# Hybrid decoder trunk: a silu behind a cast, an adaLN load behind a group's loads, two columns beside one output tile

## The chip, the cores and the metric

The kernel runs as one program on one core of a Trainium2 chip. The metric is the device time of one execution in microseconds (us). Before the change the median of three runs is 1824.08 us, from 1823.46 to 1824.4.

The core has five engines that take instructions from queues of their own, each in its program's order: TensorE (PE, matrix products; PEld are its weight loads), VectorE (DVE), ScalarE (ACT), GpSimd (POOL) and SyncE (SP). They wait for each other by semaphores. In this kernel SP and POOL mainly issue DMAs, whose packets share 16 DMA engines.

## The reference, cut to what matters

Two layers, each a SwiGLU feed-forward (FFN), a token mixing, and a second FFN; D = 1024, 512 tokens, all in float32. Only the FFNs (w_in 1024 x 5632, w_out 2816 x 1024) and the adaLN modulation are touched; the mixing is left out here:

```python
c_act = jax.nn.silu(c)
for l in range(DEPTH):
    mod = (c_act @ w_ada[l] + b_ada[l]).reshape(B, N_MOD, D_MODEL)
    sh1, sc1, gt1, sh2, sc2, gt2, sh3, sc3, gt3 = [mod[:, i, None, :] for i in range(N_MOD)]
    hn = rms_norm(h, g_ffn1[l]) * (1.0 + sc1) + sh1
    h = h + 0.5 * (1.0 + gt1) * swiglu(hn, w_ffn1_in[l], w_ffn1_out[l])
    ...
    hn = rms_norm(h, g_ffn2[l]) * (1.0 + sc3) + sh3
    h = h + 0.5 * (1.0 + gt3) * swiglu(hn, w_ffn2_in[l], w_ffn2_out[l])

def swiglu(x, w_in, w_out):
    gate, up = jnp.split(x @ w_in, 2, axis=-1)
    return (jax.nn.silu(gate) * up) @ w_out
```

## The kernel before

**Products.** A float32 weight `w` is split into two parts that PE takes at its fast rate: `wH`, a rounded copy that ACT makes (L130), and `wL = w - wH`, a subtraction on DVE (L132). Activations are split in the same way (hnH and hnL, actH and actL, comH and comL). Each product is three matmuls: H by H, L by H, H by L (L118 to L120, or L414 to L416).

**An FFN** (`ffn`, L333) has 22 hidden tiles of 128, in pairs 0 to 10. They are worked in two groups, pairs 0 to 5 and pairs 6 to 10; after each group the output projection adds that group's share to the residual h.

- The first pairs are *classical*: for each of their tiles PE makes the gate (`pg`) and the up product (`pu`), ACT applies silu to the gate (L495), DVE multiplies (L497), and the result is split. There are two such pairs, four in the first FFN of layer 0.
- Beside these tiles DVE forms sums and differences of the rows and column halves of hn, called P1, P2, T3 and T4 (`combine`). Each is a tile `q` that is split at once: cast to comH on ACT, subtraction to comL on DVE. `when` says beside which tile each is made.
- The other pairs (`pair_in`) save multiplications in the manner of Strassen: each makes products of sums of weight blocks with those sums of rows, 24 matmuls of 256 columns each. A pair loads the blocks A(1,0), as `sum0` or `sum1` by turns, with A(1,1) added to it by an accumulating DMA on POOL (L366); A(0,0) as `first`; A(0,1) as `wraw`, also called a12; A(0,0) again as `third`, with A(1,0) added by POOL; and A(1,1) as `wraw`. DVE adds `first` and later `wraw` into the sum (L356). The product with P2 goes into the accumulator `ps_d` only when ACT has copied it out (`s`, L440). In ACT's queue the cast of `third` and the copy `up` (L436) stand ahead of that copy. The product T4 of each pair is put off into the next pair.
- An output tile i (eight in group 0; six and the last two in group 1) multiplies the group's hidden tiles by two loaded pieces of w_out (w1o or w2o, 384 KB in group 0 and 320 KB in group 1). In group 0 the pieces go into `wraw` buffers or into `sum0`.

**adaLN beside it.** The matrix w_ada is too large to go through PE: a column block of 128 x 1024 is loaded by POOL (L202, `wada`, 512 KB) and DVE multiplies it by `crep`, silu(c) repeated over the partitions, and sums along the row (L188). `ada_steps` does a few of them beside each output tile. The `wada` tiles share the buffers `first`, `third` and `sum1` with the pairs' weights: the first pair of group 1 can load its own blocks only when the dots that read these buffers are done. `crep` is loaded by SP (L192) and goes through silu on ACT (L193), once in each FFN.

**What sets the order.** A scheduler fixes each engine's order of instructions when the program is built, by priority in the order of the code and by its own estimate of times. `tc.issue_after(x)` makes what is issued inside it stand behind instruction x. SP and POOL issue DMAs in order: one that waits for its buffer holds up all behind it.

Of the kernel before, what the change touches and what calls it, by code (L numbers as in the profile page):

```python
# [8 lines left out]
F32 = mybir.dt.float32  # L9
F32R = mybir.dt.float32r  # L10
I32 = mybir.dt.int32
AF = mybir.ActivationFunctionType
# [5 lines left out]
P = 128  # L18
D = 1024
# [40 lines left out]
def trunk_kernel(ctx, tc, ins, out, layers=L, phases=("ffn1", "mix", "ffn2")):  # L60
    nc = tc.nc
# [11 lines left out]
    act, mm = nc.scalar.activation, nc.tensor.matmul  # L73

    def E(name="e", dt=F32):
        return sp.tile([P, T], dt, name=name, tag="e", bufs=4)
# [7 lines left out]
    def psmm(tags=("mm",)):  # L84
        turn[0] += 1
        return psum([P, T], "ps_mm", tags[turn[0] % len(tags)])
# [27 lines left out]
    def mm3(acc, w, k, x, sl, start, stop):  # L114

        wH, wL, xH, xL = w[0][:, k], w[1][:, k], weave(x[0][:, sl]), weave(x[1][:, sl])
        acc = paired(acc)
        mm(acc, wH, xH, start=start, stop=False)  # L118
        mm(acc, wH, xL, start=False, stop=False)  # L119
        latest["large"] = mm(acc, wL, xH, start=False, stop=stop)  # L120

    latest = {}

    def queue_behind(name):
        return tc.issue_after(latest[name].ins) if name in latest else nullcontext()

    def split(hi, lo, src, behind=None):
        a, d = behind or (None, None)
        with queue_behind(a):
            nc.scalar.copy(hi, src)  # L130
        with queue_behind(d):
            return nc.vector.tensor_sub(lo, src, hi.bitcast(F32))  # L132

# [31 lines left out]
    def prm(l, name):  # L165
        a, b = PAR[name]
        return par[:, l, a:b]
# [15 lines left out]
    ada_turn = [0]  # L183
    todo = [(l, i, k) for l in range(layers) for i in range(9) for k in range(KD)][2 * KD :]

    def ada_dot(out_, w, crep):

        stt(w, w, 1.0, crep, ALU.mult, ALU.mult, accum_out=out_)  # L188

    def ada_crep(pool):  # L190
        c = pool.tile([P, D], F32, name="crep", tag="crep", bufs=1)
        nc.sync.dma_start(c, ins["crep"])  # L192
        act(c, c, AF.Silu)  # L193
        return c

    def ada_steps(pool, crep, n, behind=None):

        cols = []
        for l, i, k in todo[:n]:
            ada_turn[0] += 1  # L200
            w = pool.tile([P, D], F32, name="wada", tag=("first", "third", "sum1")[ada_turn[0] % 3], bufs=1)
            nc.gpsimd.dma_start(w, ins["wadaT"][l, i, k])  # L202
            cols.append(w)
        with tc.issue_after(behind.ins) if behind else nullcontext():
            for m, (w, (l, i, k)) in enumerate(zip(cols, todo)):
                if (l, i) not in mod:
                    mod[l, i] = const.tile([P, KD], F32, name=f"mod{l}_{i}")
                ada_dot(mod[l, i][:, k : k + 1], w, crep)
                k0 = k if m == 0 or k == 0 else k0
                if k == KD - 1 or m == len(todo[:n]) - 1:  # L210
                    v = mod[l, i][:, k0 : k + 1]
                    tt(v, v, prm(l, "b_ada")[:, i * KD + k0 : i * KD + k + 1], ALU.add)
        del todo[:n]

    def ada_until(pool, crep, l, i):
        while todo and todo[0] <= (l, i, KD - 1):
            ada_steps(pool, crep, 1)
# [60 lines left out]
    loads = []  # L278
# [43 lines left out]
    def residual(pt, i, gate, ss, sl=ALL):  # L322
        hs = inorder(h[i][:, sl])
        done = stt(hs, Woven(pt).view, gate[:, i : i + 1], hs, ALU.mult, ALU.add)
        add_ss(ss, i, sl)
        return done
# [6 lines left out]
    def ffn(l, w_in, w_pair, w_out, hn, im, ss, need, then, first, ready, coming):  # L333
# [6 lines left out]
        with tc.tile_pool(name="act", bufs=1) as ap_:  # L340
            com = {n: tuple(ap_.tile([P, 4, H2], F32R, name=x, tag="com", bufs=8) for x in ("comH", "comL")) for n in ("P1", "P2", "T3", "T4")}
            n_first = 2 if first is None else 4
            tiles = (t for t in projector([w_in[l, j, g] for j in range(2 * n_first) for g in range(2)], hn, BANKS[:3], first, 1, ready) if t is not None)
            xs, waiting, done, after, second = {}, [], [None], [None], [None]

            def flush():
                for f in waiting:
                    done[0] = f()
                waiting.clear()
# [9 lines left out]
            def raw(src, tag=None):  # L359
                w = (ap_.tile if tag else wp.tile)([P, KD, P], F32, name=tag or "wraw", tag=tag or "wraw", bufs=1 if tag else 2)  # L360
                with tc.issue_after(after[0].ins) if after[0] else nullcontext():
                    nc.sync.dma_start(w, src)
                return w

            def plus(w, src):
# [2 lines left out]
            def new_x(p):  # L368

                X = tuple(ap_.tile([P, 2, T], F32R, name=x, tag="act", bufs=12) for x in ("actH", "actL"))  # L370
                for i in range(2):
                    xs[2 * p + i] = tuple(x[:, i] for x in X)
                return X
# [97 lines left out]
            def pieces(i, g, j0, j1):  # L471
                n = (j1 - j0) // 2
                for k0 in (j0, j0 + n):
                    turn_[0] += 1
                    w = None
                    if g and (turn_[0] - 2 * KD - 1) % 6 > 1:
                        w = ap_.tile([P, KD, P], F32, name="wraw", tag="com", bufs=8)
                    elif not g and i < 7 and turn_[0] % 3 == 0:
                        w = ap_.tile([P, KD, P], F32, name="wraw", tag="sum0", bufs=1)
                    yield k0, n, load_w(w_out[l, i, :, k0 : k0 + n], n, w)  # L480


            when = {8 * (n_first == 4) + m: n for m, n in ((1, 0), (3, 1), (4, "P1"), (5, "P2"), (6, "T3"), (7, "T4"))}
            beside = lambda m: m in when and (combine if type(when[m]) is str else whole)(when[m])
            crep = ada_crep(ap_) if n_first == 4 else None
            for g, (j0, j1) in enumerate(GROUPS):
                for p in range(j0 // 2, j1 // 2):
                    if p < n_first:
                        X = new_x(p)
                        for j in (2 * p, 2 * p + 1):  # L490
                            pg = next(tiles)
                            beside(2 * j)
                            pu = next(tiles)
                            s = E("silu")
                            act(pg.like(s), pg.view, AF.Silu)  # L495
                            for seen, part in pu.pieces(s):
                                stt(part, part, -1.0, seen, ALU.mult, ALU.mult)  # L497
                            nc.scalar.copy(xs[j][0], s)
                            behind = tt(xs[j][1], s, xs[j][0].bitcast(F32), ALU.subtract)
                            beside(2 * j + 1)  # L500
                            if n_first == 4:
                                ada_steps(ap_, crep, (0, 0, 4, 4, 0, 3, 0, 0)[j], behind)
                    else:
                        after[0] = None if g or p > n_first + 1 else loads[-2]
                        pair_in(p)
                        after[0] = None
                flush()
                if g and ss is not None:

                    act(E("none")[:, :1], xs[j1 - 1][0][:, :1].bitcast(F32), AF.Sqrt, bias=vals["eps"], scale=0.0)  # L510
                if todo and not crep:
                    with tc.issue_after(loads[-1].ins):
                        crep = ada_crep(ap_)
                if g == 0:
                    cg = small_.tile([P, KD], F32, name="cg", tag="cg")
                    if n_first == 4:
                        ada_until(ap_, crep, l, im + 2)
                k1 = 0
                for i in range(KD - 2 * g):
                    if i < 7 - g:  # L520
                        many = 3 if not g else (2, 3, 3, 3, 3, 2)[i] if n_first == 4 else (3, 3, 3, 2, 2, 2)[i]
                        ada_steps(ap_, crep, many, done[0])
                    if g == 0:

                        k0, k1 = k1, KD if not todo or todo[0] > (l, im + 2, KD) else todo[0][2]
                        if k1 > k0:
                            ts(cg[:, k0:k1], mod[l, im + 2][:, k0:k1], -0.5, -0.5, ALU.mult, ALU.add)
                    pt = psmm(BANKS[:3])
                    for k0_, n, w in pieces(i, g, j0, j1):
                        for k in range(n):  # L530
                            mm3(pt, w, k, xs[k0_ + k], ALL, k0_ + k == j0, k0_ + k == j1 - 1)
                    done[0] = residual(pt, i, cg, ss if g else None)

            n = (j1 - j0) // 2
# [860 lines left out]
    with tc.tile_pool(name="first", bufs=1) as fp:  # L1395
        hn, first = begin(fp)
    ready = ()
    for n, (l, p) in enumerate(seq):
# [20 lines left out]
        else:  # L1419
            w, need = ("w1", (l, 7)) if p == "ffn1" else ("w2", (l + 1, 1))  # L1420
            ready = ffn(l, ins[w + "i"], ins[w + "p"], ins[w + "o"], hn, im, nss, need, then, first, ready, coming)
        first = None
# [86 lines left out]
```

## Time and profile before

| what | us |
|---|---|
| median of three runs (1823.46 to 1824.4) | 1824.08 |
| the profiled execution | 1835.1 |
| its span, from first to last instruction | 1833.3 |
| PE busy | 1786.3 |
| DVE busy | 1353.5 |
| ACT busy | 843.6 |

The mean granted clock of TensorE was 0.993 of full speed. In the time line the first FFN of layer 0 takes roughly 40 to 380 us, the second 595 to 955, the first of layer 1 930 to 1265, the second 1497 to 1833; the mixings lie between.

How to read the rows: a row of the time line has its start in us from the start of the span, its length in us, engine, line, operation, and what is written from what; "[1.33 <-DVE wL L132]" says that the engine idled for 1.33 us just before it, and what ended that. A row of the waits has the waiting engine, tile and line, the one waited for, and us in total, times, longest. A row of DMA issues has the engine that issued it, how many, KB, and median us from issue to landing. A row of windows has the stretch, its length, busy time and count of each engine (PE, PEld, DVE, ACT, POOL), granted clock, DMA share and GB/s.

### The profile page before, as it was taken

The page shows a single profiled execution, that of the slowest core. Times are in us where ns is not written, and L with a number is a line of the kernel's source. Part 1 is how long each engine was busy: PE and PEld are TensorE (multiplying, and loading weights), DVE is VectorE, ACT ScalarE, POOL GpSimd, SP SyncE. Part 2 cuts the span into 40 slices and gives each one's busy share as a digit, 9 for nine tenths or more (in the row PEclk, how much of TensorE's full clock was granted, in tenths as well). Part 3 has the DMA queues.
Part 4 walks back from the last instruction along what each step waited for, and adds up shares of the span by engine and source line. Part 5 has one row for each costly group of instructions (what it writes and reads, how often), then busy time and mean ns, then how long its engine had stood idle before and what let it go on. Part 6 is the DMA issues. An engine that isn't in the chain of part 4 may idle for free. (4 is left out here: it accounts for less than half of the span.)

```text
span 1833.3 us, 33697 instructions
## 1 busy us (share of the span) xinstructions
PE 1786.3 (97%) x13856; PEld 1627.6 (89%) x13856; DVE 1353.5 (74%) x2185; ACT 843.6 (46%) x1296; POOL 140.6 (8%) x222
## 2 busy tenths in 40 slices
PE   8999999999999999999999998999999999999999
PEld 6889899987778899889899988999877798999998
DVE  6687677877766787678878785787686677874862
ACT  4444255374444464156345523543644445533551
POOL 0101110101000001100100011010000000110000
PEclk8999999999999999999999999999999999999999
DMA  8667876613113476886737677674321126775742
GB/s 314 220 185 235 270 207 200 235 64 102 53 37 98 124 213 193 277 215 186 239 118 195 175 277 218 197 213 154 108 66 50 59 78 183 194 223 142 202 139 70
DMA packets 91548, 308.36 MB, mean 168 GB/s; under 512 B 10432, under 2 KB 11200, under 8 KB 90368
## 3 DMA queue, kind: packets, MB, share of 16 engines
q1 hardware_dynamic: 62496, 201.58, 32.2%
q0 software_dynamic: 28896, 104.61, 22.7%
q8 instruction: 109, 1.79, 0.4%
q14 instruction: 47, 0.39, 0.1%
HBM read 302.74 MB, written 3.41 MB: 167 GB/s over the span
## 5 line engine op out<-in xcount | busy, mean ns | idle before, releaser
L130 ACT CAST wH<-wraw 128x1024 fp32r<-128x1024 f32 (+2 forms) x292 | 266.1, 917 | 450.0 <-PE ps_mm L119 206.1
L132 DVE TENSOR_TENSOR wL<-wraw,wH 128x1024 fp32r<-128x1024 f32 (+2 forms) x292 | 308.3, 1060 | 106.1 <-ACT wH L130 105.1
L120 PE MATMUL ps_mm<-actH,wL 128*128 128x512 f32 (+1 forms) x784 | 280.8, 358 | 2.8 <-DVE wL L132 2.8
L118 PE MATMUL ps_mm<-actH,wH 128*128 128x512 f32 (+1 forms) x784 | 281.0, 358 | 0.0
L119 PE MATMUL ps_mm<-actL,wH 128*128 128x512 f32 (+1 forms) x784 | 280.5, 358 | 0.0
L118 PE MATMUL ps_mm<-hnH,wH 128*128 128x512 f32 (+1 forms) x760 | 267.2, 359 | 6.4 <-ACT hnH L130 2.9
L119 PE MATMUL ps_mm<-hnL,wH 128*128 128x512 f32 (+1 forms) x760 | 266.7, 353 | 0.3
L120 PE MATMUL ps_mm<-hnH,wL 128*128 128x512 f32 (+1 forms) x760 | 264.9, 351 | 0.6 <-DVE wL L132 0.6
L414 PE MATMUL ps_d<-comH,wH 128*128 128x256 f32 x816 | 225.4, 276 | 0.3 <-ACT s L440 0.3
L415 PE MATMUL ps_d<-comL,wH 128*128 128x256 f32 x816 | 225.1, 276 | 0.0
L416 PE MATMUL ps_d<-comH,wL 128*128 128x256 f32 x816 | 225.0, 276 | 0.0
L188 DVE SCALAR_TENSOR_TENSOR wada<-wada,crep 128x1024 f32<-128x1024 f32 x140 | 167.8, 1221 | 54.9 <-DMA wada<-in_wadaT 54.8
L132 DVE TENSOR_TENSOR wL<-sum,wH 128x1024 fp32r<-128x1024 f32 x102 | 125.0, 1225 | 71.0 <-ACT wH L130 70.9
L118 PEld LDWEIGHTS ps_mm<-hnH,wH 128*128 128x128 f32 x760 | 143.4, 192 | 29.3 <-issue 7.6
L120 PEld LDWEIGHTS ps_mm<-actH,wL 128*128 128x128 f32 x784 | 148.7, 190 | 20.6 <-DVE wL L132 3.8
L119 PEld LDWEIGHTS ps_mm<-actL,wH 128*128 128x128 f32 x784 | 148.7, 190 | 16.6
L118 PEld LDWEIGHTS ps_mm<-actH,wH 128*128 128x128 f32 x784 | 148.7, 190 | 16.5
L120 PEld LDWEIGHTS ps_mm<-hnH,wL 128*128 128x128 f32 x760 | 145.9, 192 | 15.8 <-DVE wL L132 1.1
L119 PEld LDWEIGHTS ps_mm<-hnL,wH 128*128 128x128 f32 x760 | 145.9, 192 | 15.7 <-DVE hnL L273 1.0
L414 PEld LDWEIGHTS ps_d<-comH,wH 128*128 128x128 f32 x816 | 157.4, 193 | 0.9 <-ACT s L440 0.9
L415 PEld LDWEIGHTS ps_d<-comL,wH 128*128 128x128 f32 x816 | 157.4, 193 | 0.0
L416 PEld LDWEIGHTS ps_d<-comH,wL 128*128 128x128 f32 x816 | 157.3, 193 | 0.0
(366 smaller groups left out, 3748.4 us busy)
## 6 DMA issues: line engine op xcount, KB each, us to landing
wada<-in_wadaT POOLq DMA_DIRECT2D x128, 512.0 KB, 4.8
wraw<-in_wmi SPq DMA_DIRECT2D x40, 512.0 KB, 3.5
wraw<-in_w2p SPq DMA_DIRECT2D x36, 512.0 KB, 4.2
wraw<-in_w1p SPq DMA_DIRECT2D x32, 512.0 KB, 4.3
wraw<-in_w1o SPq DMA_DIRECT2D x32, 384.0 KB, 5.2
wraw<-in_w2o SPq DMA_DIRECT2D x32, 384.0 KB, 4.2
wraw<-in_w1i SPq DMA_DIRECT2D x20, 512.0 KB, 4.3
wraw<-in_w1o SPq DMA_DIRECT2D x32, 320.0 KB, 3.7
```

Of the source, the lines that this page charges most:

```text
L118: mm(acc, wH, xH, start=start, stop=False)
L119: mm(acc, wH, xL, start=False, stop=False)
L120: latest["large"] = mm(acc, wL, xH, start=False, stop=stop)
L130: nc.scalar.copy(hi, src)
L132: return nc.vector.tensor_sub(lo, src, hi.bitcast(F32))
L188: stt(w, w, 1.0, crep, ALU.mult, ALU.mult, accum_out=out_)
L414: mm(acc, wH, xH, start=start and i + k == 0, stop=False, skip_group_check=True)
L415: mm(acc, wH, xL, start=False, stop=False, skip_group_check=True)
L416: mm(acc, wL, xH, start=False, stop=k == 3, skip_group_check=True)
```

## The change

Three edits, none of which adds or removes a product:

1. In the classical tiles beside which a `combine` stands, silu of the gate is issued behind the ACT cast of that sum.
2. `crep` is loaded behind the last weight load of the pairs of group 0, and no longer behind the last load recorded before (a classical tile's weights). In the first FFN, which makes its `crep` at the start, nothing changes.
3. Beside output tile 6 of group 0 two adaLN columns are worked and not three, in the buffers `third` and `sum1` only. The column left over goes to group 1: the counts of columns by tile become (3,3,3,3,3,2) in the first FFN and (3,3,3,3,2,2) in the others. In the second FFN of layer 1 only eight columns are left to do, all at tiles 0 to 2, so that this edit does not reach it.

```diff
     def split(hi, lo, src, behind=None):
         a, d = behind or (None, None)
         with queue_behind(a):
-            nc.scalar.copy(hi, src)
+            latest["cast"] = nc.scalar.copy(hi, src)
...
-    def ada_steps(pool, crep, n, behind=None):
+    def ada_steps(pool, crep, n, behind=None, tags=("first", "third", "sum1")):
...
-            w = pool.tile([P, D], F32, name="wada", tag=("first", "third", "sum1")[ada_turn[0] % 3], bufs=1)
+            w = pool.tile([P, D], F32, name="wada", tag=tags[ada_turn[0] % len(tags)], bufs=1)
...
-                    nc.sync.dma_start(w, src)
+                    latest["raw"] = nc.sync.dma_start(w, src)
...
                             beside(2 * j)
+                            held = tc.issue_after(latest["cast"].ins) if type(when.get(2 * j)) is str else nullcontext()
                             pu = next(tiles)
                             s = E("silu")
-                            act(pg.like(s), pg.view, AF.Silu)
+                            with held:
+                                act(pg.like(s), pg.view, AF.Silu)
...
                 if todo and not crep:
-                    with tc.issue_after(loads[-1].ins):
+                    with tc.issue_after(latest["raw"].ins):
                         crep = ada_crep(ap_)
...
-                        many = 3 if not g else (2, 3, 3, 3, 3, 2)[i] if n_first == 4 else (3, 3, 3, 2, 2, 2)[i]
-                        ada_steps(ap_, crep, many, done[0])
+                        many = 3 - (i == 6) if not g else (3, 3, 3, 3, 3, 2)[i] if n_first == 4 else (3, 3, 3, 3, 2, 2)[i]
+                        ada_steps(ap_, crep, many, done[0], *[("third", "sum1")][: i == 6])
```

In the changed file lines from 495 on stand two lower (silu is L497 there, the split of its result L500).

ACT at the end of the classical tiles of the second FFN of layer 0, before. `comH<-q` are the casts of P1, P2 (the "x2"), T3 and T4; `sum_6723` is the first pair's sum, `crep<-crep` the silu of c.

```order
L130 COPY wH<-sum_6723 128x1024
L495 ACTIVATE silu<-ps_mm 128x512
L130 COPY comH<-q 128x1024 x2
L130 COPY wH<-first 128x1024
L498 COPY actH<-silu 128x512
L130 COPY comH<-q 128x1024
L495 ACTIVATE silu<-ps_mm 128x512
L130 COPY comH<-q 128x1024
L193 ACTIVATE crep<-crep 128x1024
L130 COPY wH<-sum_6723 128x1024
```

The same place of the changed kernel:

```order
L130 COPY wH<-sum_6724 128x1024
L130 COPY comH<-q 128x1024
L497 ACTIVATE silu<-ps_mm 128x512
L130 COPY comH<-q 128x1024
L130 COPY wH<-first 128x1024
L500 COPY actH<-silu 128x512
L130 COPY comH<-q 128x1024
L497 ACTIVATE silu<-ps_mm 128x512
L130 COPY comH<-q 128x1024
L130 COPY wH<-sum_6724 128x1024
```

The cast of P1 and the silu have changed places, and the silu of c is gone from ahead of the second `wH<-sum`; the second silu stood behind T3's cast already. The same swap is made in the first FFN of layer 0 and the second of layer 1; in the first of layer 1 P1's cast came first before.

ACT in the last pair of group 0 of the same FFN, changed kernel; before, the rows are the same without the one of `crep`:

```order
L130 COPY wH<-wraw 128x1024
L419 COPY actH<-up 128x2x256
L436 COPY up<-ps_f 128x512
L193 ACTIVATE crep<-crep 128x1024
L130 COPY wH<-third 128x1024
L440 COPY s_7454<-ps_d 128x512
L130 COPY wH<-sum_7390 128x1024
```

The silu of c now stands 45 instructions further down on ACT, ahead of the cast of `third` and the copy of `ps_d`.

SP at the end of group 0 of the same FFN, before. `sum_8137` and `sum_8337` are the sums of pairs 6 and 7 (`sum0`, `sum1`), the first `wraw<-in_w2p` is pair 6's a12:

```order
L362 DMA sum_8137<-in_w2p 128x1024
L284 DMA wraw<-in_w2o 128x768 x2
L362 DMA wraw<-in_w2p 128x1024
L362 DMA third<-in_w2p 128x1024
L362 DMA sum_8337<-in_w2p 128x1024
L362 DMA first<-in_w2p 128x1024
L362 DMA wraw<-in_w2p 128x1024
```

Changed:

```order
L362 DMA sum_8135<-in_w2p 128x1024
L284 DMA wraw<-in_w2o 128x768
L362 DMA first<-in_w2p 128x1024
L284 DMA wraw<-in_w2o 128x768
L362 DMA wraw<-in_w2p 128x1024
L362 DMA sum_8335<-in_w2p 128x1024
L362 DMA third<-in_w2p 128x1024
L362 DMA wraw<-in_w2p 128x1024
```

`first` of pair 6 goes ahead of the last piece of w2o and of a12, and `third` comes behind pair 7's sum. On POOL the accumulating loads change in the same way (pair 7's sum, then `third`). DVE's two dots read `sum1` first and `third` second. The first FFN of layer 1 is ordered alike; in the first FFN of layer 0 `first` moves in the same way, but `third` keeps its place ahead of the sum.

## The prediction

> **What bounds the kernel now.** I read the busy times first, then what TensorE waits for over the whole span, then the stretches round the edited places by engine.
>
> ```profile
> span 1833.3 us, 33697 instructions
> PE 1786.3 (97%) x13856; PEld 1627.6 (89%) x13856; DVE 1353.5 (74%) x2185; ACT 843.6 (46%) x1296; POOL 140.6 (8%) x222
> PE ps_g L416 <- DVE wL L132: 6.4, 5, 1.6
> ```
>
> TensorE is busy for 97% of the span, and the change neither adds nor removes a matmul. Whatever it wins must come out of the 47 us in which PE is idle, at the three kinds of place it touches. The last row (us in total, times, longest) shows what much of that idle time looks like: PE waits for one half of a split weight, the subtraction on DVE (wL); elsewhere for the cast on ACT (wH). Nothing large can come of this, and little can go wrong unless a wait that is hidden now comes out.
>
> The profiled execution took 1835.1 us round its span of 1833.3, 0.6% above the median of 1824.08. The terms below are microseconds of that profiled execution; I subtract them from the median unscaled, since 0.6% of a few microseconds is nothing.
>
> **Part 1, the cast of P1 ahead of silu.** The order of instructions differs by one swap on ACT, in three of the four FFNs. Second FFN of layer 0, ACT, then DVE, then PE:
>
> ```profile
> 628.67 0.59 ACT L495 ACTIVATE silu<-ps_mm 128x512 f32<-128x512 f32 x1
> 629.16 1.03 ACT L130 CAST comH<-q 128x1024 fp32r<-128x1024 f32 x1
> 630.23 1.23 DVE L132 TENSOR_TENSOR comL<-q,comH 128x1024 fp32r<-128x1024 f32 x1 [2.98 <-ACT comH L130]
> 640.26 0.38 PE L416 MATMUL ps_f<-comH,wL 128*128 128x256 f32 x1 [1.33 <-DVE wL L132]
> 1543.25 0.38 PE L416 MATMUL ps_f<-comH,wL 128*128 128x256 f32 x1 [0.72 <-DVE wL L132]
> ```
>
> DVE stands idle for 2.98 us until comH of P1 is there, and then works almost without a pause up to the wL for which PE waits 1.33 us. silu holds ACT for 629.16 - 628.67 = 0.49 us ahead of that cast. With the cast first, the whole DVE chain moves up by 0.49, and so does PE's restart: -0.5. silu itself ends about 1 us later (the cast), but what reads it on DVE stands behind comL, an addition and a wL. The second FFN of layer 1 has the same chain, with 0.72 us of wait to give (last row): -0.5 again. In the first FFN of layer 0 the wait of the first pair hangs on the third sum and a load, not on P1: 0. Bounds: 0 (if the wait behind takes it back) to -0.5 each.
>
> **Part 2, crep's load and silu go from the first pair to the last of group 0.** The load stands on SP behind the last weight load of pair 5; the silu on ACT between a copy (`up`) and the cast of `third`. It happens in three FFNs.
>
> ```profile
> 642.64 1.06 ACT L193 ACTIVATE crep<-crep 128x1024 f32<-128x1024 f32 x1 [3.39 <-DMA crep<-in_crep]
> 643.64 1.05 ACT L130 CAST wH<-sum 128x1024 fp32r<-128x1024 f32 x1
> 642.39 1.22 DVE L356 TENSOR_TENSOR sum<-sum,first 128x1024 f32<-128x1024 f32 x1
> crep<-in_crep SPq DMA_DIRECT2D x1, 512.0 KB, 3.5
> 695.79 0.33 SPq L362 DMA_DIRECT2D wraw<-in_w2p  x1
> wraw<-in_w2p SPq DMA_DIRECT2D x1, 512.0 KB, 4.1
> 702.31 0.58 ACT L440 COPY s<-ps_d 128x512 f32<-128x512 f32 x1
> 703.90 0.28 PE L414 MATMUL ps_d<-comH,wH 128*128 128x256 f32 x1
> ```
>
> At the old place ACT idles 3.39 us for the load and then does the silu, but the cast behind it (643.64) could not have begun before DVE's addition of `sum` and `first` ended at 642.39 + 1.22 = 643.61. So the silu costs 0.03 there today; what its removal is worth is that Part 1's half microsecond is not eaten by a silu that still waits for its load. I count 0 for it by itself. (Bound below: -0.3 each.)
>
> At the new place it must fit in ahead of the copy at 702.31, for which the product at 703.90 (P2 of pair 5) waits, since the copy clears its accumulator. The load would be issued about 0.33 us behind 695.79, at 696.1. Alone it takes 3.5 us (its own row) and lands at 699.6; behind the 4.1 us of the load ahead, at one more 512 KB, I take 701.2. Then silu 1.0 (from 642.64 to 643.64), the cast of `third` (0.95 to the next start, like the other casts in a row) and the copy 0.58 end at 701.2 + 1.0 + 0.95 + 0.58 = 703.7: 0.2 us to spare. So 0, but the thinnest cover of this change, three times.
>
> **Part 3, the seventh output tile of group 0 takes two adaLN columns.** A column is a 512 KB load on POOL's queue into one of three buffers (first, third, sum1) and a dot on DVE; the first pair of group 1 then loads its own weights into the same buffers, each when the dot that read it is done. The PE order is unchanged. In the first FFN of layer 0:
>
> ```profile
> 215.88 1.23 DVE L188 SCALAR_TENSOR_TENSOR wada<-wada,crep 128x1024 f32<-128x1024 f32 x1 [1.34 <-DMA wada<-in_wadaT]
> 217.03 0.95 DVE L132 TENSOR_TENSOR wL<-wraw,wH 128x768 fp32r<-128x768 f32 x1
> 218.04 0.48 PE L120 MATMUL ps_mm<-actH,wL 128*128 128x512 f32 x1 [0.97 <-DVE wL L132]
> ```
>
> The third dot is the one that holds wL of the last tile. Without it wL starts at least 1.15 us sooner (the dots' distance), and PE's 0.97 with its refill goes: -1.1. Against it: `first`, which now loads ahead of the last piece of w1o, can make the second column later. If both dots slide to where the last stood, the gain is 0; that is this term's other end.
>
> In the two middle FFNs the same place is a chain of waits. Second FFN of layer 0: the two later dots on DVE, PE's waits in pair 6 (us in total, times, longest), P2's first matmul, two rows of ACT, then landing times of loads (us from issue): the plain one of `third`, POOL's accumulating one of sum1, and POOL's two, first and second, in the first FFN:
>
> ```profile
> 774.27 1.23 DVE L188 SCALAR_TENSOR_TENSOR wada<-wada,crep 128x1024 f32<-128x1024 f32 x1 [2.69 <-DMA wada<-in_wadaT]
> 775.86 1.23 DVE L188 SCALAR_TENSOR_TENSOR wada<-wada,crep 128x1024 f32<-128x1024 f32 x1 [0.35 <-DMA wada<-in_wadaT]
> PE ps_g L416 <- DVE wL L132: 1.6, 1, 1.6
> PE ps_d L416 <- DVE wL L132: 0.8, 1, 0.8
> PE ps_d L414 <- ACT wH L130: 0.7, 1, 0.7
> PE ps_g L414 <- ACT wH L130: 0.5, 1, 0.5
> 792.23 0.28 PE L414 MATMUL ps_d<-comH,wH 128*128 128x256 f32 x1
> 789.43 1.04 ACT L130 CAST wH<-third 128x1024 fp32r<-128x1024 f32 x1
> 790.85 0.58 ACT L440 COPY s<-ps_d 128x512 f32<-128x512 f32 x1
> third<-in_w2p SPq DMA_DIRECT2D x1, 512.0 KB, 5.3
> sum<-in_w2p POOLq DMA_DIRECT2D x1, 512.0 KB, 9.2
> third<-in_w1p POOLq DMA_DIRECT2D x1, 512.0 KB, 5.7
> sum<-in_w1p POOLq DMA_DIRECT2D x1, 512.0 KB, 7.4
> ```
>
> Today `first` comes last of the three, so pair 6 waits for it (0.7 and 0.8 in ps_d, then 0.5 and 1.6 in ps_g, further down the same chain). With `first` free before the last tile's columns, all that goes. What is late next is `third`: its buffer now waits for the last of two dots instead of the first of three, and in these two FFNs POOL adds to it only behind `sum1`. ACT's queue makes that count: the cast of `third` stands ahead of the copy (790.85) on which P2 (792.23) waits. The last tile's own wait for wL, behind the last dot, I keep, because `first` takes the lost column's place in the traffic and the dots' order is turned (the buffer loaded second is read first).
>
> So: both dots end between 774.27 + 1.15 + 1.15 = 776.6 and 775.86 + 2.3 = 778.2; I take 777.5. Plain load of `third`: between 3.5 (crep's) and 5.3, say the 4.1 of the load above, to 781.6. Then, 0.2 later, the accumulate, queued behind sum1's: the nearest row is the one that already stands second on POOL with `first` out of the way, in the first FFN: 7.4 (ends: the 5.7 of the one ahead of it there, and 9.2). It lands at 781.8 + 7.4 = 789.2; from the cast to the copy's end takes 791.43 - 789.43 = 2.0, so P2 starts at 791.2 instead of 792.23: -1.0. Ends: 776.6 + 3.5 + 0.2 + 5.7 + 2.0 = 788.0, less than the 792.2 - 0.7 - 0.8 - 0.5 - 1.6 = 788.6 that PE's own work allows, so -3.6; and 778.2 + 5.3 + 0.2 + 9.2 + 2.0 = 794.9, +2.7.
>
> First FFN of layer 1: its last dot, PE's waits from 1104 to 1135, P2, and the granted clock of the stretch behind (the number ahead of the last two):
>
> ```profile
> 1111.65 1.22 DVE L188 SCALAR_TENSOR_TENSOR wada<-wada,crep 128x1024 f32<-128x1024 f32 x1 [0.16 <-DMA wada<-in_wadaT]
> PE ps_d L414 <- ACT wH L130: 1.8, 1, 1.8
> PE ps_g L416 <- DVE wL L132: 1.6, 1, 1.6
> PE ps_d L416 <- DVE wL L132: 0.8, 1, 0.8
> PE ps_g L414 <- ACT wH L130: 0.5, 1, 0.5
> 1129.52 0.42 PE L414 MATMUL ps_d<-comH,wH 128*128 128x256 f32 x1
> 1129.00:1132.50 3.50, 3.50 (x18) 3.50 (x18) 3.20 (x3) 1.05 (x1) 0.00 (x0) 0.51 0.38 131
> ```
>
> By the same steps: dots end at 1111.65 + 2.3 = 1113.9, `third` is loaded at 1118.0, its accumulate lands at 1118.2 + 7.4 = 1125.6, P2 starts at 1127.6 instead of 1129.52: -1.9. Ends: -4.7 (the four waits) and, with 9.2, 1118.2 + 9.2 + 2.0 = 1129.4, about 0.
>
> After these waits the clock was 0.51 for 3.5 us, which costs 3.5 x 0.49 = 1.7. By the sum, waits of over a microsecond remain at both places, so I leave one such window in the sum: 0, with ends -1.7 and +1.7. The Trainium skill (TensorE: Matmul & The Clock Gate, Part 1) grants half speed only after an idle window of about 3.4 us; by it neither place would ever be slowed, and the sum would be 1.7 better. The trace speaks against it: the half clock follows waits of 0.5 and 1.6 us with work between them.
>
> The column taken away is dotted in group 1, one tile with three instead of two. Price 1.2 of DVE at each of three tiles; cover, in the second FFN of layer 0 at that tile:
>
> ```profile
> 902.50:909.00 6.50, 6.50 (x32) 5.70 (x31) 5.17 (x10) 1.72 (x3) 1.06 (x2) 1.00 0.85 259
> ```
>
> DVE (5.17 of 6.50) has 1.3 free, PE is full, so 0; without that cover, up to 1.2 a place.
>
> **Sum.** -1.1 - 0.5 - 1.0 - 1.9 - 0.5 = -5.0: 1824.1 - 5.0 = **1819.1 us**. The resolution of this measurement I put at 0.2%, 3.65 us.
>
> **Rivals.** *All gaps go.* `third` lands as early as its lower ends say, PE then waits so little that the half clock, which follows those waits today, stays away: -1.1 - 0.5 - 3.6 - 4.7 - 0.5 - 1.7 = -12.1, 1812.0. For it: nothing here shows which of 5.7, 7.4 and 9.2 holds. Against: three loads and two accumulates still share the same engines. The skill (DMA: Bandwidth & Descriptors, Issuing engines are not separate DMA queues) says just that; 9.2 here beside 7.4 in the first FFN agrees.
>
> *third takes first's place.* If its accumulate lands at 792.2 - 2.0 = 790.2 and 1127.5, both middle places give nothing: -1.1 - 0.5 - 0.5 = -2.1, 1822.0, and a second half-clock window makes it 1823.7: no change.
>
> *crep comes late, slower.* The silu waits for its load with the cast of `third` and the copy behind it. From a landing 0.2 us past 701.2 on, each further microsecond costs PE one, three times. At the 9.2 us of the worst load above it lands at 705.3, 3.9 too late each: 1819.1 + 11.7 = 1830.8. Slower than before by 3.65 needs 8.65 / 3 = 2.9 each. For it: the traffic of the pair's loads stands just ahead. Against: that load took 4.1 and SP has nothing else then.
>
> *The change does nothing* at the silu (order alike where it was already so): worth 1.0, inside the range.
>
> **Chances.** Forecast and its neighbourhood (-3.7 to -9) 0.46, all gaps 0.14, `third` in `first`'s place 0.28, crep 0.12. So faster 0.60, same 0.28, slower 0.12. Range: from all gaps, 1812, to just past `third` with two windows, 1825; outside are crep's rival and little else.
>
> **What would show it.** Right: at the last tile of the first FFN no wait of PE for wL; at the first pairs of both second FFNs PE's waits shorter by half a microsecond and no crep on ACT; in pair 6 of the middle FFNs no wait for wH of `first`, ACT's cast of `third` released by its DMA at about 789.2 and 1125.6, P2 right behind the copy. Wrong: ACT idle at crep's silu in pair 5 with PE waiting for the copy behind it; `third` landing past 790.2 and 1127.5; PE waiting for wL in group 1's tiles of three columns.

## The result: slower, and the profile after

The changed kernel takes 1842.19 us (median, 1837.09 to 1845.11) against 1824.4 us of the kernel before in the same comparison. The ratio on record is 1.0074, with a 95% interval from 1.0058 to 1.0091; it is not the quotient of these two medians, which is 1.0098, so the loss is some 13 to 18 us. Forecast was 1819.1 us, faster. The prediction was wrong in sign.

Times of one program scatter here more than the small effects: the kernel before alone had medians of 1824.4, 1828.2, 1827.8 and 1828.5 us in the four comparisons of this document. So each experiment is told by its ratio to the runs of before made beside it.

The head of the profile after, and the waits of PE over the whole span that are new in it (us in total, times, longest):

```profile
span 1841.1 us, 33707 instructions
PE 1790.1 (97%) x13856; PEld 1630.6 (89%) x13856; DVE 1353.3 (74%) x2186; ACT 842.3 (46%) x1296; POOL 140.6 (8%) x222
PE ps_d L414 <- ACT s L440: 11.4, 4, 5.3
PE ps_ss L254 <- ACT sq L235: 3.2, 3, 1.8
```

The busy times are nearly those of before; PE's 3.8 us more fit the half clock below. PE's longest sum of waits is now one that held 0.3 us in the profile before: on ACT's copy of `ps_d` (L440), the copy ahead of P2. Two of its four waits make up 9.9 us. They stand in pair 6 of the second FFN of layer 0 and of the first of layer 1. In the second FFN of layer 0, the time line of DVE, SP, POOL, ACT and PE, and the time from issue to landing of the accumulate of `third`:

```profile
774.81 1.23 DVE L188 SCALAR_TENSOR_TENSOR wada<-wada,crep 128x1024 f32<-128x1024 f32 x1 [8.77 <-DMA wada<-in_wadaT]
775.97 1.22 DVE L188 SCALAR_TENSOR_TENSOR wada<-wada,crep 128x1024 f32<-128x1024 f32 x1
776.07 0.33 SPq L362 DMA_DIRECT2D sum<-in_w2p  x1
777.22 0.33 SPq L362 DMA_DIRECT2D third<-in_w2p  x1
780.15 0.87 POOL L366 DMA_DIRECT2D sum<-in_w2p  x1 [16.32 <-DVE h L324]
782.81 0.86 POOL L366 DMA_DIRECT2D third<-in_w2p  x1 [1.78 <-DMA third<-in_w2p]
third<-in_w2p POOLq DMA_DIRECT2D x1, 512.0 KB, 8.2
791.09 1.04 ACT L130 CAST wH<-third 128x1024 fp32r<-128x1024 f32 x1 [6.78 <-DMA third<-in_w2p]
792.51 0.59 ACT L440 COPY s<-ps_d 128x512 f32<-128x512 f32 x1
793.15 0.58 PE L414 MATMUL ps_d<-comH,wH 128*128 128x256 f32 x1 [5.29 <-ACT s L440]
```

DVE idles for 8.77 us until the column that was loaded second (the one in `sum1`'s buffer) has landed, and then does both dots without a pause: the first of them reads the buffer of `sum1`, and the column in `third`'s buffer, already there, stands behind it. So `third` is asked for at 777.22 only. Its accumulate is issued at 782.81, behind that of sum1, but what POOL waited for was `third`'s own plain load (the 1.78 in that row). ACT stands 6.78 us in front of the cast with the copy queued behind it. The first FFN of layer 1, and the stretches behind both waits (the number ahead of the last two is the granted clock):

```profile
1134.92 0.58 PE L414 MATMUL ps_d<-comH,wH 128*128 128x256 f32 x1 [4.62 <-ACT s L440]
793.00:796.50 3.50, 3.35 (x15) 3.35 (x16) 1.61 (x2) 1.04 (x2) 0.00 (x0) 0.50 0.53 152
1134.90:1138.40 3.50, 3.48 (x16) 3.48 (x17) 1.48 (x2) 0.92 (x1) 0.00 (x0) 0.50 0.49 150
796.50:798.50 2.00, 2.00 (x12) 2.00 (x11) 0.00 (x0) 0.00 (x0) 0.85 (x1) 0.50 0.86 236
1138.40:1139.80 1.40, 1.40 (x9) 1.40 (x9) 0.00 (x0) 0.00 (x0) 0.56 (x1) 0.50 0.89 222
798.60:802.00 3.40, 3.40 (x33) 3.40 (x32) 1.76 (x3) 2.58 (x3) 0.84 (x1) 1.00 0.95 158
```

Behind the waits PE runs at half clock up to 798.5 and 1139.9, some 5.4 and 5.0 us of work, which costs 2.7 and 2.5 more. The waits and the clock make 5.3 + 4.6 + 2.7 + 2.5 = 15.1 us. This is not yet the loss, since the kernel before waited in pair 6 too, for `first`. Counted by the starts of the same matmuls (each matmul of one profile against its counterpart in the other, as PE's order is unchanged), from ahead of the last tile to behind the half clock, the change loses 2.4 us in the second FFN of layer 0 and 1.4 in the first of layer 1 against the first profile of the kernel before, and 6.1 and 2.5 against its second profile (the next section), of 7.8 and 15.2 us in all. Group 1 of the first FFN with the norm behind it makes another 3.4 and 2.7 us.

### The profile page after: what moved, and what is told of

It is laid out like the page before. It is cut to its first block, busy times and chain, and to the rows that moved or that the text cites. A ratio compares the mean times of both kernels' runs of the same rounds, so it can differ in the third digit from the quotient of the medians.

```text
span 1841.1 us, 33707 instructions
## 1 busy us (share of the span) xinstructions
PE 1790.1 (97%) x13856; PEld 1630.6 (89%) x13856; DVE 1353.3 (74%) x2186; ACT 842.3 (46%) x1296; POOL 140.6 (8%) x222
## 3 DMA queue, kind: packets, MB, share of 16 engines
HBM read 302.74 MB, written 3.41 MB: 166 GB/s over the span
## 5 line engine op out<-in xcount | busy, mean ns | idle before, releaser
L130 ACT CAST wH<-sum 128x1024 fp32r<-128x1024 f32 x102 | 106.9, 1048 | 125.8 <-PE ps_f L415 42.1
```

The source lines that it names most:

```text
L130: latest["cast"] = nc.scalar.copy(hi, src)
```

## The experiments

**The kernel before, again.** No edit.

> The kernel before, unchanged. Its profiled execution took 1835.1 us and its median 1824.1, while the changed kernel's two numbers are 1843.0 and 1842.2. Theory A (the sites in the two traces are the whole story): times between 1823 and 1835 as before, ratio 1.000, and a new profile loses the same time at the same places. Theory B (the profiled execution of before was an unlucky one): a new profile has a span near 1822, and some 11 us of waits that the first profile has are gone from it.

Ratio 0.9994 (0.9985 to 1.0003), span 1825.9 us instead of 1833.3. Pair 6 of the second FFN of layer 0, PE's waits from 778 to 790, all of them:

```profile
PE ps_g L416 <- DVE wL L132: 1.6, 1, 1.6
```

The waits of 0.7, 0.8 and 0.5 us that hung on `first` are not there; in the first FFN of layer 1 they are (1.53, 0.77 and 0.52), but the 3.5 us behind them ran at full clock. So part of what I meant to win was a property of one execution: the one profiled first took 1835.1 us, 11 above the median, this one 1827.7, close to its median of 1828.0. Theory B holds for some 5 of the 7.4 us by which the spans differ: by the starts of the same matmuls 3.4 from the last tile to pair 6 of the second FFN of layer 0, and 1.7 of clock; the remainder lies in many small differences.

**The three edits apart.** The silu alone (the line that records the cast is left out here):

```diff
...
+                            held = tc.issue_after(latest["cast"].ins) if type(when.get(2 * j)) is str else nullcontext()
...
+                            with held:
+                                act(pg.like(s), pg.view, AF.Silu)
```

> Only the silu behind the cast of the rows' sum. Theory A: PE's wait at the first pair of the second FFN of layer 0 (1.33 us) and of layer 1 (0.72) shrinks by 0.5 each, so -1.0 us. Rival: the product of the later pairs takes the half microsecond back, 0. Slower than +1 us would say that the held silu itself keeps a PSUM bank too long.

Ratio 0.9991 (0.9977 to 1.0004): a gain of 1.6 us that the interval doesn't tell from none. PE's wait at `ps_f` in the first pairs is 0.2 us in its profile; in the two of the kernel before it was 2.1 and 1.1. The sign agrees with theory A, the size isn't settled.

crep alone (the line that records the last weight load is left out):

```diff
...
-                    with tc.issue_after(loads[-1].ins):
+                    with tc.issue_after(latest["raw"].ins):
                         crep = ada_crep(ap_)
```

> Only crep's load and silu moved to the last pair of group 0. Theory A, from the changed kernel's trace, where the load landed 5.0 to 6.6 us after its issue: PE waits for the copy behind it in pair 5 by 0.3, 0 and 1.4 us, and nothing is gained at the first pair: +1.7 us, with PE's wait on the copy (ps_d L414 <- ACT s L440) the only new one there. Rival: the silu is what made the changed kernel slow, by waits in all three FFNs: +6 us or more.

Ratio 1.0009 (0.9998 to 1.0019), +1.6 us, at the edge of what can be told. Two of the three last pairs wait for the copy now (0.95 and 1.17 us; the second is shown), and in the changed kernel's own profile the third does, by 1.25 us, with ACT in front of the silu:

```profile
1041.74 0.38 PE L414 MATMUL ps_d<-comH,wH 128*128 128x256 f32 x1 [1.17 <-ACT s L440]
1612.16 1.06 ACT L193 ACTIVATE crep<-crep 128x1024 f32<-128x1024 f32 x1 [2.07 <-DMA crep<-in_crep]
1614.68 0.38 PE L414 MATMUL ps_d<-comH,wH 128*128 128x256 f32 x1 [1.25 <-ACT s L440]
```

This fits theory A, a small loss at the place foreseen, though the interval just reaches 1. The rival, a loss of 6 us or more by crep's silu, is out.

The seventh tile alone (two columns there, one more in group 1, the buffers in the change's order; the lines for the counts and the tuple are those of the change and left out here):

```diff
...
-                        ada_steps(ap_, crep, many, done[0])
+                        ada_steps(ap_, crep, many, done[0], *[("third", "sum1")][: i == 6])
```

> Only the two columns beside the seventh output tile, with one more in group 1. Theory A, by the steps between the two traces: first FFN -1.1 + 1.2 + 2.0, second FFN of layer 0 -1.1 + 1.1 + 2.4 (half clock) + 0.7, first FFN of layer 1 +1.5 - 0.9 + 0.9 + 0.9, so about +7.6 us or more. Rival: this edit gains 4 us as predicted (-1.1 - 1.0 - 1.9) and the loss lies in crep's silu.

1842.69 us, ratio 1.0070 (1.0053 to 1.0087), where the whole change has 1.0074: this edit is the whole loss, as far as the intervals tell. P2 waits for the copy 3.63 and 5.42 us.

**What in it.** First, the same edit with the one difference that the first of the two columns always takes the buffer of `third`:

```diff
-            w = pool.tile([P, D], F32, name="wada", tag=tags[ada_turn[0] % len(tags)], bufs=1)
+            w = pool.tile([P, D], F32, name="wada", tag=tags[m] if tags else ("first", "third", "sum1")[ada_turn[0] % 3], bufs=1)
```

> Two columns beside the seventh tile as in the change, but in all FFNs the column in the buffer of third is loaded, read and given back first, so that third's accumulate stands ahead of sum1's on POOL. Silu and crep stay as before. Theory A (what costs is that third waits for the dot that is read last and then stands second on POOL): PE's waits on the copy (3.8 and 5.6 us) and the half clock behind them go, at least 9 us less than the run with the change's order (1842.7): 1833 or less. Rival B (any two-column version lets five loads collide, whatever their order): within 3 us of 1842.7.

1824.89 us, ratio 0.9978 (0.9956 to 1.0000). The order of two columns moves the kernel by 0.9%. Rival B is out: it isn't the number of loads.

Then the change's order with the left-over column not computed at all:

> The change at the seventh tile with its own order of buffers, but the column taken away is left out altogether (one column of the modulation in each of the three FFNs is not computed and set to zero), and group 1 has its old counts. Theory A: group 1 pays for the extra column at the norm behind it (steps of 0.4 + 0.4 + 1.75 us in the first FFN, 0.3 and 0.33 + 1.85 in the others), so some 4 to 5 us less than 1842.7, about 1838. Rival: group 1's cover is as wide as predicted, less than 1 us of difference. Most of the loss must stay in either case.

1824.93 us, ratio 0.9983 (0.9967 to 0.9999), 17.8 us less than the edit with it and far more than either theory allowed. The reason is mostly in the order, not in group 1: the buffers rotate with a running count of columns, so that one column less in the first FFN turned the order round in the second, where `third` came first. In the first FFN of layer 1 (two less) it was the change's order again. The run thus holds both orders. P2's first matmul in either FFN, and the 3.5 us behind it:

```profile
785.65 0.38 PE L414 MATMUL ps_d<-comH,wH 128*128 128x256 f32 x1 [1.72 <-ACT s L440]
1121.98 0.58 PE L414 MATMUL ps_d<-comH,wH 128*128 128x256 f32 x1 [4.89 <-ACT s L440]
785.60:789.10 3.50, 3.45 (x30) 3.45 (x31) 1.51 (x2) 1.41 (x3) 0.00 (x0) 1.00 0.68 243
1122.00:1125.50 3.50, 3.50 (x16) 3.50 (x17) 1.44 (x2) 0.87 (x1) 0.00 (x0) 0.50 0.50 162
```

`third` first: 1.72 us and full clock. sum1 first: 4.89 us and half clock behind.

Third, two columns in `third` and `first`, so that `sum1` is free early (the tuple of the edit above is then `("third", "first")`):

> Two columns, in third (read first) and first (read second); sum1 is free early, so pair 7's sum and its accumulate are out of the way before third's. Theory A: no wait on the copy, and the waits for first of the kernel before come back in part: 1826 to 1834. Rival B: the two-column version costs as much as the change, over 1839.

1831.2 us, ratio 1.0020 (1.0006 to 1.0033), within theory A's span: no wait on the copy among PE's largest, `first` late as before, and a wait of 4.40 us for the last tile's wL in the first FFN, which no theory named. Fourth, three columns as before in the order `first`, `third`, `sum1`:

> Three columns as before, and all else as before; only the buffers beside the seventh tile are taken in the order first, third, sum1 in all three FFNs, as the first FFN has it already. Theory A: in the two middle FFNs the waits for first (0.7 + 0.8 + 0.5 + 1.6 and 1.8 + 0.8 + 0.5 + 1.6 in the first profile, about 3 and 5 in the second) go, and third, second in line, comes in time for its cast: 3 to 8 us faster than before. Rival: third's cast takes first's place ahead of the copy, and nothing is gained.

1831.85 us, ratio 1.0024 (1.0010 to 1.0038): a miss. The waits for `first` went, but the last tile of the first FFN of layer 1 now waits 3.45 us for its wL. With three columns this order is no better than the one before; by the interval it is a little slower.

**The column in group 1.** `third` first, the left-over column not computed, order kept equal to that of the run above with `third` first:

> Third first as in e5, and the column taken away is left out altogether in the three FFNs (set to zero, not computed), group 1 with its old counts. Against e5 (1824.9) it shows the price of the extra column in group 1 alone. Theory A: the norm's waits of 2.2 and 1.0 us go, and 0.3 to 0.7 in the second FFN of layer 0: 3 to 4 us less than e5. Rival (as predicted, the column is hidden): the same as e5 within 1 us.

1822.34 us, ratio 0.9964 (0.9949 to 0.9978), 2.6 us less than with the column, nearer theory A's 3 to 4 than none; but the two intervals overlap, so the size is not settled. The place shows in the traces: the norm behind the first FFN, where `ps_ss` sums the squares of h. PE's wait for the last square there, with the column and without it:

```profile
364.70 0.59 PE L254 MATMUL ps_ss<-ones_r,sq 128*128 128x1 f32 x2 [2.63 <-ACT sq L235]
361.53 0.38 PE L254 MATMUL ps_ss<-ones_r,sq 128*128 128x1 f32 x2 [0.21 <-ACT sq L235]
```

In the five profiles with a third column at tile 0 of group 1 this wait is 1.75 to 2.63 us; without it, it is never over 0.65.

**The whole change with `third` first.** All three edits, and only this difference:

```diff
-            w = pool.tile([P, D], F32, name="wada", tag=tags[ada_turn[0] % len(tags)], bufs=1)
+            w = pool.tile([P, D], F32, name="wada", tag=tags[ada_turn[0] % 3 if len(tags) == 3 else m], bufs=1)
```

> The whole change, all three edits, with the one difference that beside the seventh tile the column in third's buffer is always taken first. Theory A: this one difference takes back nearly all of the change's loss: 1824 to 1829 instead of 1842. Rival: the edits make each other worse (crep's load among them), and it stays over 1833.

1824.29 us, ratio 0.9981 (0.9966 to 0.9995): 17.9 us less than the change. The same rows as in the profile after, second FFN of layer 0:

```profile
771.57 1.23 DVE L188 SCALAR_TENSOR_TENSOR wada<-wada,crep 128x1024 f32<-128x1024 f32 x1 [7.49 <-DMA wada<-in_wadaT]
773.45 1.23 DVE L188 SCALAR_TENSOR_TENSOR wada<-wada,crep 128x1024 f32<-128x1024 f32 x1 [0.65 <-DMA wada<-in_wadaT]
772.83 0.33 SPq L362 DMA_DIRECT2D third<-in_w2p  x1
776.73 0.87 POOL L366 DMA_DIRECT2D third<-in_w2p  x1 [14.59 <-DMA third<-in_w2p]
783.50 1.05 ACT L130 CAST wH<-third 128x1024 fp32r<-128x1024 f32 x1 [1.71 <-DMA third<-in_w2p]
785.57 0.38 PE L414 MATMUL ps_d<-comH,wH 128*128 128x256 f32 x1 [0.22 <-ACT s L440]
```

The plain load goes out after the first dot, 4.4 us earlier than in the change (772.83 against 777.22), the accumulate 6.1 us earlier, and P2 waits 0.22 us where it waited 5.29. Its first matmul starts 7.6 us earlier; at the last tile just before (775.60 against 778.12) this run was 2.5 us ahead, so some 5.1 us are the place itself, and the half clock behind it comes on top. The cast of `third` stands 7.6 us earlier (783.50 against 791.09): 4.4 of that is the earlier request, 1.7 a shorter plain load and 1.5 a shorter accumulate. By the starts of the same matmuls, the last tile and pair 6 with the clock behind make 8.2 us of difference in this FFN and 8.5 in the first of layer 1, 16.7 of the 17.2 us by which the two spans differ.

**A version that beats the kernel before.** Silu as in the change, crep and the first FFN as before, `third` first in the two middle FFNs, and both left-over columns beside tiles of group 1 of the second FFN of layer 0, whose norm doesn't need them:

```diff
...
+                        two = not g and i == 6 and n_first == 2
+                        many = 3 - two if not g else (2, 3, 3, 3, 3, 2)[i] if n_first == 4 else (3, 3, 3, 2 + (l == 0), 2 + (l == 0), 2)[i]
+                        ada_steps(ap_, crep, many, done[0], ("third", "sum1") if two else ())
```

> A version meant to beat both: the silu edit; two columns (third first, then sum1) beside the seventh tile of the two middle FFNs only; the two columns left over both go to group 1 of the second FFN of layer 0, behind which no norm needs them; the first FFN and crep as before. Theory A (third's place in line and the column ahead of the norm are what cost): the run with third first stood at 0.9978, without its 2.2 us of norm wait in the first FFN and 1.0 in the first of layer 1 and with the silu's 1 to 2 us it is 0.995, some 1819. Rival: the gains at these places are only given back later, 0.998 or more.

1822.12 us, ratio 0.9967 (0.9955 to 0.9980): 6 us faster than before, with less than theory A's 9. The intervals do not tell it from the whole change with `third` first (0.9981). Then the same version with the first FFN changed too:

> As the combined version, and the first FFN too has two columns beside its seventh tile; the one left over goes beside a classical tile there (four instead of three at the sixth). Theory A: PE's wait for wL of the last tile of group 0 (1.0 us) goes and the classical tile hides a fourth dot: 0 to -1 us against the combined version. Rival: the fourth column there comes out as a wait of the tile, +1 us.

1828.57 us, ratio 1.0000 (0.9987 to 1.0012): a miss, and worse than the rival had it. In its profile the last tile of group 0 of the first FFN waits for wL all the same (1.62 us), and P2 in the first FFN of layer 1 waits 2.11 us for the copy. The first Strassen pair behind the classical tiles waits 3.3 us (0.49, 0.77, 1.10 and 0.96) where the combined version waits 1.5. Why the copy is late in layer 1, with the order there as in the combined version, stays open.

## Why the prediction was wrong, point by point

**What the sum missed.** By the starts of the same matmuls in the two profiles, before and after, the change loses 7.8 us where -5.0 was said. Of these 12.8 us the last tile and pair 6 with the half clock behind make 3.4 and 3.3 in the two middle FFNs, the tiles of group 1 and the norms behind them 5.0 in three FFNs, crep's place 1.9; the silu's places gave 1.4 more than said, and 0.6 are scattered.

**The step that failed is the start of P2 in pair 6.** The prediction named the mechanism (third's buffer waits for the last dot, its accumulate stands behind sum1's, its cast stands ahead of the copy) and put P2 1.0 us and 1.9 us earlier than before. In the profile after it starts 0.9 us later in the second FFN of layer 0 (793.15), and 5.4 us later in the first of layer 1 (1134.92), of which PE had lost 5.0 ahead of the last tile. PE stands 5.29 and 4.62 us in front of it. Three sizes add up in the second FFN of layer 0: the dots ended at 777.2 (said: 777.5), but the accumulate, which needs the plain load, was issued at 782.8 and not at 781.8, and took 8.2 us and not 7.4. It landed at 791.0 where I said 789.2, past the 790.2 that I had named as the point from which nothing is left. In layer 1 the steps from the end of the dots (1119.6) were 5.5 us to the accumulate instead of 4.3, and 7.6 for it instead of 7.4.

**The base was wrong as well.** The sum was made against waits for `first` of 3.6 us in one execution; the second profile of the same program lacks most of them at one of the two places. With PE ahead by what those waits cost, a late `third` is a wait from the first microsecond. The rival (*third* takes *first*'s place) was therefore the case, but priced at no change: its floor of nothing held only where `first` had been as late as `third`. That the profiled execution stood 11 us above the median was known, and its terms were taken off the median all the same.

**The half clock.** Left at one stretch, as before; measured were two, 2.7 and 2.5 us. They follow from the waits.

**The last tile.** First FFN: the wait of 0.97 us is gone, as said. Second FFN of layer 0: its wait went from 1.84 to 0.78. First FFN of layer 1: a new one of 1.32 us, not foreseen; the column read first is the one that lands last.

**The column in group 1 was put at nothing, and costs some 2.6 us** (with `third` first; the size is not settled). I compared DVE's busy time with PE's in one tile. PE's wait for wL in a tile of three columns, named beforehand as a sign of being wrong, is there: 0.99 us in the first FFN of the profile after, none before. What the column also moves is the chain behind it: the buffers of group 1's columns are given back 2.4 to 2.9 us later in the first FFN, and with that begin the loads of the mixing's weights into these buffers. ACT waits for the last of them ahead of the last square of the norm. In the profile after, that load on SP, ACT's cast and the square:

```profile
357.42 0.33 SPq L545 DMA_DIRECT2D wraw<-in_wmi  x1
362.83 1.05 ACT L130 CAST wH<-wraw 128x1024 fp32r<-128x1024 f32 x1 [2.14 <-DMA wraw<-in_wmi]
365.62 0.42 ACT L235 ACTIVATE sq<-h 128x256 f32<-128x256 f32 x1 [1.75 <-DVE h L324]
```

In the profile before the same load was issued at 354.97, and the cast began at 359.70, after a wait of 0.70.

**crep** was named the thinnest cover, at 0.2 us to spare, and entered as 0. Its load took 5.0 to 6.6 us to land where 5.1 was taken, and alone it measured +1.6 us for the three places, at the edge of what can be told. The place was right, the landing was put too short.

**silu**: -1.0 was said, and -1.6 measured with an interval that reaches past 0. Neither confirmed nor refuted.

## What to carry to other kernels

Where buffers are shared by turns, the number of loads is one thing and which buffer comes free first is another. Read which load the next stage needs first and which of two columns DVE reads first; a rotation by a running count decides that anew in every stage, and one column more or less anywhere upstream turns it round.

A wait that the change removes must be seen in more than one profile before it is counted, and the profile should be of an execution near the median. And when something is costed as hidden since an engine has time to spare, follow the buffer and not the engine: who loads into it next, and what stands behind that load's consumer.

## What the runs showed of the hardware

The length of a single wait does not settle whether the half clock follows. It followed the waits on the copy of 3.63, 4.62, 4.89, 5.29 and 5.42 us, and also the 2.63 us at the norm shown above (its matmul takes 0.59 us, the other 0.38). Behind 1.72 us the clock stayed at 1.00. In the profile of the combined version, PE waits as long at the same matmul of both mixings; behind the wait of layer 1 the clock is 0.50, behind that of layer 0 it is 1.00:

```profile
1392.69 0.53 PE L637 MATMUL ps_t<-TT,X 64*64 64x64 f32 x21 [2.30 <-DVE X L964]
1393.35:1396.76 3.41, 3.41 (x42) 1.93 (x35) 3.37 (x7) 0.00 (x0) 0.00 (x0) 0.50 0.19 41
503.66 1.16 PE L637 MATMUL ps_t<-TT,X 64*64 64x64 f32 x64 [2.29 <-DVE X L964]
502.47:505.88 3.41, 2.22 (x69) 1.74 (x71) 3.35 (x7) 0.00 (x0) 0.00 (x0) 1.00 0.02 5
```

What the traces show instead is a fixed step. In each of the 14 profiles all changes of the clock lie whole multiples of 3.413 us apart. I divided each profile into these steps and added up the gaps between matmuls in each, from 45 us to shortly before the end. Every one of the 24 steps at full clock with 1.97 us of gaps or more is followed by half clock; of the 80 with 1.2 to 1.96 us 12 are; of those with less, none. (The ends of matmuls are modelled in the trace, so the border is rough.)

This also answers the case of the prediction, the 0.51 behind waits of 0.5 and 1.6 us. The steps there, two of the first profile of the kernel before and then three of the second:

```profile
1125.66:1129.07 3.41, 1.27 (x9) 0.89 (x8) 3.38 (x4) 2.85 (x4) 0.00 (x0) 1.00 0.41 143
1129.07:1132.48 3.41, 3.41 (x18) 3.41 (x17) 3.13 (x3) 1.05 (x1) 0.00 (x0) 0.50 0.38 131
1119.25:1122.66 3.41, 1.93 (x15) 1.54 (x14) 2.42 (x3) 3.41 (x5) 0.00 (x0) 1.00 0.47 156
1122.66:1126.07 3.41, 2.76 (x24) 2.76 (x25) 3.38 (x4) 1.46 (x2) 0.00 (x0) 1.00 0.15 36
1126.07:1129.48 3.41, 3.41 (x33) 3.41 (x32) 1.89 (x3) 2.33 (x3) 0.00 (x0) 1.00 0.91 345
```

The waits are the same in both. In the first profile they fall into one step, and PE is busy for 1.27 of 3.41 us in it; in the second the border at 1122.66 divides the longer one, and PE is busy for 1.93 and 2.76. So these 1.7 us hang on where the steps lie in an execution, which is luck.

The Trainium skill (TensorE: Matmul & The Clock Gate, Part 1) gives half speed after an idle window of about 3.4 us that runs freely. The length of the steps agrees with it; but here a window needn't be idle throughout, since 2.1 us of 3.41 were enough. The prediction read the rule as one unbroken wait; so read, the trace did speak against it.
